# Ties, accumulator tiles and a layer border in a two-layer decoder trunk

## The chip, the core and the metric

The kernel runs on one core of one Trainium2 chip. The metric is device time in microseconds (us) of one execution, the median over a few runs. Engines are named as in the profile: PE is the tensor engine's matmul, PEld its weight load, DVE the vector engine, ACT the scalar engine, POOL the GpSimd engine, SP the engine that issues most of the loads.

## The reference

Two layers over x (256 positions x 2048 features), each `x <- LayerNorm(alpha * x + mixer(x))`:

```python
def reference(x, ...):
    for layer in range(DEPTH):                      # DEPTH = 2
        if layer % 2 == 0:
            h = ssd_moba_mixer(x, in0_w, ..., out0_w)
        else:
            h = s5_mixer(x, in1_w, ..., w_glu, out1_w)
        x = layer_norm(DEEPNORM_ALPHA * x + h, ln_g[layer], ln_b[layer])
    return x

def ssd_moba_mixer(x, w_in, conv_w, ...):
    z, xbc, dt, q, k, v, gate = jnp.split(x @ w_in, SPLITS0, axis=-1)
    xbc = jax.nn.silu(causal_depthwise_conv(xbc, conv_w, conv_b))
    ...                                             # SSD scan, causal attention
    return jnp.concatenate([y_a, y_b], axis=-1) @ w_out

def s5_mixer(x, w_in, ...):
    u, gate = jnp.split(x @ w_in, 2, axis=-1)
    y = jax.nn.gelu(s5_ssm(u, ...))                 # diagonal complex scan
    ga, gb = jnp.split(y @ w_glu, 2, axis=-1)
    return (ga * jax.nn.sigmoid(gb) * jax.nn.silu(gate)) @ w_out
```

All in float32. Nearly all arithmetic is in five projections: in0, out0, in1, glu, out1.

## The kernel before

**Split products.** Every float32 operand of a projection is split in two: a high part (`wh`, `xh`, rounded to the matmul's format) and the low rest (`wl`, `xl`). A product is the sum of three matmuls: high x high, high x low, low x high. Weights come in units of 256 rows x 512 columns (512 KB), 431 whole ones and a first one in parts. `split_to` (L210) loads a unit (`raw`, SP's queue), rounds it on ACT (L230) and subtracts on DVE (L232). `raw`, `wh` and `wl` have four buffers each, so a unit can be split once PE is done with the unit four before it.

**Products.** `product` (L288) runs over the units of one 512-column chunk. It calls `split_to` three units ahead, issues the unit's matmuls, and calls `pump`. Kind "w" (`wmm`, L273; 24 matmuls of 256 columns a unit, the weights stationary) gives a transposed result; kind "x" (`xmm`, L266; 12 matmuls of 512 columns a unit) a straight one. In kind "w" the two halves of the accumulator take turns within a unit (o = 0, 1 in the first bank, o = 2, 3 in the second). In order: 2 products for B and C, 4 for the convolution's x, 4 for z, 16 for attention, 4 of double length for out0, 8 for in1, 8 for glu, 4 for out1.

**Accumulators.** `banks` (L261) makes one tile of two PSUM banks for each product, of two tags in turn; `Pair` carries the tile and its halves. A product can start when the work that reads the tile of two products before is done.

**Spread work.** What follows from a product (convolution taps, rotary, scores, gates) is appended to `jobs`; longer-running work (SSD heads, the S5 tables' block jobs, the S5 scan) to `back`. `pump` (L242) calls a few of them after each unit, so that all of a product's `jobs` are traced during the next one. Each engine's final order is made by a planner that walks the program with a timing model: it takes work in traced order, but draws later work forward where it is ready and the engine would be idle. `tc.issue_after(ins)` makes the instructions of its block that run on the engine of `ins` come behind `ins` in that order. So far only `y_split` (L1175) uses it, against the split traced last, and the border's `step`.

**Early stage.** Product 3 to 6 are the convolution's x. After each, four taps (L498 on ACT, three L501 on DVE each) read the accumulator. Beside them run the softplus of dt (POOL, L451 to L462), the trigonometric and table jobs (L547 to L608) and, from far later in traced order, the first block job (`bars` L645 to L651, `efs` L665 to L675).

**Layer border.** `product_apart` (L323) computes out0's last chunk: ten units for both halves of the positions (t = 0, 1; o in the code), then the last six units first for t = 0 (36 matmuls) and then for t = 1. After each half, `after0` (L1019) queues its `first`: `res0` (L955: residual L960, statistics L961), `norm_stats` (L977 to L980, square root on ACT) and `step` (L994) for chunk 0; for t = 0 chunk 1 as well. A `step` takes 512 columns: L1003 and L1006 scale and shift on DVE, four transposes on PE (L351), the high part by a copy on ACT (L1014, tile C), the low part by a subtraction on DVE (L1015, tile F). Then come 60 small matmuls on a zero tile (`warm`, L356), and the first product of in1, whose unit k needs the columns 256k to 256k + 255 of both t. The remaining steps are traced inside that product (`later`), the one for t = 1, chunk 1 ahead of unit 1.

**End.** out1's last chunk uses `product_apart` too, with all eight units apart; `res1` (L1246: L1248, L1249) reads each half.

Of the kernel before, what the change touches and what calls it, by code (L numbers as in the profile page):

```python
# [9 lines left out]
F32 = mybir.dt.float32  # L10
# [6 lines left out]
P = 128  # L17
S = 256
# [7 lines left out]
WARM1 = 60  # L26
# [11 lines left out]

class Pair(list):
    def __init__(self, both, parts):  # L40
        super().__init__(parts)
        self.both = both

# [121 lines left out]
def trunk(tc, io, out):  # L165
# [8 lines left out]
    with ExitStack() as top:  # L174
# [32 lines left out]
        last = {}  # L207
        keep = [None, range(0)]

        def split_to(i):  # L210
            while nsplit[0] <= min(i, len(units) - 1):
                n = nsplit[0]
                if n in early:
                    early.pop(n)()
                raw = st.tile([P, UK, 512], F32, tag="raw", name=nm("raw"))
                if n == 0:
                    wh = st.tile([P, UK, 512], F32R, tag="wh", name=nm("wh"))
                    wl = st.tile([P, UK, 512], F32R, tag="wl", name=nm("wl"))
                    for k in range(UK):
# [10 lines left out]
                last["a"] = A.activation(wh, raw, AF.Copy)  # L230
# [10 lines left out]

        def pump(left):  # L242
            n = -(-len(jobs) // max(left, 1))
            for _ in range(n):
                jobs.popleft()()
            if back:
                goal[1] += len(back) / max(goal[0] - unit[0], 1)
            while back and goal[1] >= 1.0:
                back.popleft()()
                goal[1] -= 1.0  # L250

        def drain():
            while jobs:
                jobs.popleft()()

        def finish():
            while back:
                back.popleft()()
# [14 lines left out]
        def wmm(ps, u, nu, hl, wpair):  # L273
            pv = [p.rearrange("p (f n) -> p f n", n=S) for p in ps]
            wh, wl = wpair
            steps = [(j, o) for j in range(UK) for o in range(4)]
            if u == nu - 1:
                steps = [(j, o) for o in range(4) for j in range(UK)]
            for j, o in steps:
                first, end = u == 0 and j == 0, u == nu - 1 and j == UK - 1  # L280
                (xh, xl), k = hl(u * UK + j)
                sl = slice(o * P, o * P + P)
                for i, (l, r) in enumerate(((wh, xh), (wh, xl), (wl, xh))):
                    T.matmul(pv[o // 2][:, o % 2, :], l[:, j, sl], r[:, k, :],  # L284
                             start=first and i == 0 and o % 2 == 0, stop=end and i == 2 and o % 2 == 1,
                             skip_group_check=True)

        def product(kind, hl, nu=CU, prelude=None):  # L288
            ps = banks()
            for u in range(nu):  # L290
# [4 lines left out]
                if kind == "w":  # L295
                    wmm(ps, u, nu, hl, wpair)
# [26 lines left out]
        def product_apart(hl, nu, nk, after):  # L323
# [25 lines left out]
        def transpose4(dst, srcs):  # L349
            for i, s in enumerate(srcs):  # L350
                T.transpose(dst[:, i * P : i * P + P], s, ident)  # L351
# [630 lines left out]
        with ExitStack() as lt:  # L982
# [11 lines left out]
            def step(t, i, stats=None):  # L994
                if not x1t:
                    x1t["h"] = big("C", [P, KT, S], F32R)
                    x1t["l"] = big("F", [P, KT, S], F32R)
                sl = slice(512 * i, 512 * i + 512)
                xv = x1n[:, t, sl]
                with ExitStack() as pin:  # L1000
# [5 lines left out]
                    op2 = V.scalar_tensor_tensor(xv, xv, mr0[:, t, 2:3], rows[1][:, sl], op0=OP.mult, op1=OP.add)  # L1006
                tail["v"] = op2
                px = aux()
                transpose4(px, [x1n[:, t, (4 * i + f) * P : (4 * i + f) * P + P] for f in range(4)])
                pv = px.rearrange("p (f c s) -> p f s c", f=4, s=4)  # L1010
                fs = slice(4 * i, 4 * i + 4)
                hv = x1t["h"][:, fs, :].rearrange("p f (s c) -> p f s c", s=4)[:, :, :, 32 * t : 32 * t + 32]
                lv = x1t["l"][:, fs, :].rearrange("p f (s c) -> p f s c", s=4)[:, :, :, 32 * t : 32 * t + 32]
                A.activation(hv, pv, AF.Copy)  # L1014
                low = V.tensor_tensor(lv, pv, hv.bitcast(F32), op=OP.subtract)  # L1015
# [24 lines left out]
            first1 = product("w", x1hl, prelude=lambda u: [step(t, i) for t, i in later.get(u, [])])  # L1040
# [3 lines left out]
        with ExitStack() as l1:  # L1044
# [130 lines left out]
            def y_split(j):  # L1175
# [17 lines left out]
            for j in range(8):  # L1193
# [3 lines left out]
                else:  # L1197
                    jobs.append(lambda ps=ps, j=j: A.activation(sg1[:, :, 512 * j - 2048 : 512 * j - 1536], ps.both, AF.Silu))
# [10 lines left out]
            def glu_jobs(ps, j):  # L1209
                d = {}  # L1210

                def gate():
                    sb = w1("gt", [P, 2, 256])
                    A.activation(sb, ps.both[:, :, 256:512], AF.Sigmoid)
                    t1 = d["t"] = w1("p1", [P, 2, 256])
                    V.tensor_tensor(t1, ps.both[:, :, 0:256], sb, op=OP.mult)
# [81 lines left out]
```

## Time and profile before

| | us |
|---|---|
| median of 3 runs | 1376.59 |
| lowest, highest | 1375.08, 1376.98 |
| the profiled execution's own time | 1375.91 |
| its span in the profile | 1374.1 |
| its mean granted PE clock | 0.992 |

| engine | busy, us | share of the span |
|---|---|---|
| PE | 1346.6 | 98% |
| PEld | 1214.5 | 88% |
| DVE | 979.9 | 71% |
| ACT | 673.7 | 49% |
| POOL | 307.1 | 22% |

A line of the page's groups reads: source line, engine, operation, output <- inputs, shape, count | busy time, mean ns of one | idle time just before them and what ended it. A line of the view of waits reads: who waited <- for whom: us in total, times, longest. A row of the chain of waits or of the timeline begins with its start and its length in us; the chain follows the work that ended last back from the end. Matmuls overlap, so the pace of PE is read from starts, not from the length of one. The granted clock is the share of full speed that the tensor engine got.

### The profile page before, as it was taken

Reading aid. Unit: us, or ns where it says so; the run is one execution under the profiler, and the core shown is the slowest. Engines: PE = TensorE matmul, PEld = TensorE weight load, DVE = VectorE, ACT = ScalarE, POOL = GpSimd, SP = SyncE. Lnnn points to the kernel's source line nnn. Section 1 sums busy time; section 2 is a strip of 40 time slices with the busy share of each in tenths; the row PEclk is TensorE's granted clock in tenths of the full one; section 3 lists DMA queues with packets and bytes.
Section 4 is the critical chain, followed back from the end, with each engine's and each line's share of the span. In section 5 each row is a group of like instructions: output and inputs, shape, how many; then the busy total and the mean of one; then the engine's idle time right before and its main releaser. Section 6 shows DMA issues by size and latency. Waiting matters only on the chain.

```text
span 1374.1 us, 24912 instructions
## 1 busy us (share of the span) xinstructions
PE 1346.6 (98%) x9944; PEld 1214.5 (88%) x9944; DVE 979.9 (71%) x1548; ACT 673.7 (49%) x856; POOL 307.1 (22%) x457
## 2 busy tenths in 40 slices
PE   9996999999999999999999999899999999999996
PEld 9996999998999999999988888799977788888885
DVE  5789768888666679688768855748888846555555
ACT  5563557765554454454464434344344545444441
POOL 0157787833002002002000000023343200000001
PEclk9998999999999999999999999999999999999998
DMA  8554766555556656646756678387988766666761
GB/s 307 175 162 132 229 195 189 162 181 154 168 162 193 217 164 213 223 150 220 243 175 222 218 219 302 120 305 237 297 278 306 216 211 190 185 192 190 247 216 74
DMA packets 79204, 283.01 MB, mean 206 GB/s; under 512 B 9840, under 2 KB 10480, under 8 KB 78576
## 3 DMA queue, kind: packets, MB, share of 16 engines
q1 hardware_dynamic: 68112, 239.33, 55.4%
q0 software_dynamic: 10400, 40.90, 9.0%
q8 instruction: 78, 1.28, 0.4%
q10 hardware_dynamic: 576, 1.18, 0.2%
q14 instruction: 38, 0.31, 0.1%
HBM read 260.41 MB, written 20.97 MB: 205 GB/s over the span
## 4 chain that ended last, share of the span: by engine, by line
PE 91%; DVE 3%; DMA 2%; POOL 2%; ACT 1%; issue 1%; POOLq 0%; SPq 0%; DVEq 0%; ACTq 0%
PE main L271 42%; PE main L284 41%; DVE wl L232 1%; PE aux L351 1%; PE enc L1103 1%; PE aux L781 1%; DMA raw<-in_wo 1%; PE aux L687 1%; DMA raw<-in_wi 1%; PE aux L359 1%; DMA xr<-in_xn 1%; PE dec L1148 1%; POOL ew L461 1%; PE aux L683 1%; PE aux L861 1%
## 5 line engine op out<-in xcount | busy, mean ns | idle before, releaser
L232 DVE TENSOR_TENSOR wl<-raw,wh 128x1024 fp32r<-128x1024 f32 x431 | 540.7, 1259 | 281.2 <-ACT wh L230 275.2
L230 ACT ACTIVATE wh<-raw 128x1024 fp32r<-128x1024 f32 x431 | 455.4, 1059 | 549.4 <-PE main L271 272.5
L284 PE MATMUL main<-A,wh 128*128 128x256 f32 x1408 | 404.0, 287 | 10.3 <-DVE a L501 10.3
L284 PE MATMUL main<-A,wl 128*128 128x256 f32 x1408 | 400.8, 285 | 0.0
L284 PE MATMUL main<-B,wh 128*128 128x256 f32 x1408 | 400.2, 284 | 0.0
L284 PEld LDWEIGHTS main<-A,wh 128*128 128x128 f32 x1408 | 271.5, 193 | 11.2 <-issue 10.7
L284 PEld LDWEIGHTS main<-B,wh 128*128 128x128 f32 x1408 | 271.5, 193 | 0.3
L284 PEld LDWEIGHTS main<-A,wl 128*128 128x128 f32 x1408 | 271.5, 193 | 0.1
L271 PE MATMUL main<-wh,A 128*128 128x512 f32 x512 | 201.2, 393 | 1.7 <-DVE D L960 1.7
L271 PE MATMUL main<-wl,A 128*128 128x512 f32 x512 | 200.0, 391 | 0.0
L271 PE MATMUL main<-wh,B 128*128 128x512 f32 x512 | 199.6, 390 | 0.0
L271 PE MATMUL main<-wh,C 128*128 128x512 f32 x384 | 152.7, 398 | 0.8 <-DVE D L1248 0.8
L271 PE MATMUL main<-wl,C 128*128 128x512 f32 x384 | 149.9, 390 | 0.0
L271 PE MATMUL main<-wh,F 128*128 128x512 f32 x384 | 149.7, 390 | 0.0
L271 PEld LDWEIGHTS main<-wh,A 128*128 128x128 f32 x512 | 96.1, 188 | 22.2 <-DVE D L960 2.1
L271 PEld LDWEIGHTS main<-wh,B 128*128 128x128 f32 x512 | 96.1, 188 | 20.0
L271 PEld LDWEIGHTS main<-wl,A 128*128 128x128 f32 x512 | 96.2, 188 | 19.2
L271 PEld LDWEIGHTS main<-wh,C 128*128 128x128 f32 x384 | 72.1, 188 | 16.8 <-DVE D L1248 1.2
L271 PEld LDWEIGHTS main<-wh,F 128*128 128x128 f32 x384 | 72.1, 188 | 15.2
L271 PEld LDWEIGHTS main<-wl,C 128*128 128x128 f32 x384 | 72.1, 188 | 14.2
L284 PE MATMUL main<-C,wh 128*128 128x256 f32 x256 | 74.1, 290 | 0.7 <-ACT C L1014 0.7
L284 PE MATMUL main<-F,wh 128*128 128x256 f32 x256 | 73.5, 287 | 0.3 <-DVE F L1015 0.3
(281 smaller groups left out, 1575.6 us busy)
## 6 DMA issues: line engine op xcount, KB each, us to landing
raw<-in_wi SPq DMA_DIRECT2D x271, 512.0 KB, 4.2
raw<-in_wo SPq DMA_DIRECT2D x96, 512.0 KB, 4.2
raw<-in_wglu SPq DMA_DIRECT2D x64, 512.0 KB, 3.7
wt<-wb POOLq DMA_DIRECT2D x16, 896.0 KB, 7.7
wb<-ob POOLq DMA_DIRECT2D x16, 512.0 KB, 5.8
bc<-in_s5bc SPq DMA_DIRECT2D x16, 256.0 KB, 4.3
wb<-F POOLq DMA_DIRECT2D x16, 256.0 KB, 4.0
wb<-om POOLq DMA_DIRECT2D x16, 128.0 KB, 4.3
```

What stands on the lines that cost most here:

```text
L230: last["a"] = A.activation(wh, raw, AF.Copy)
L232: last["v"] = V.tensor_tensor(wl, raw, wh.bitcast(F32), op=OP.subtract)
L271: T.matmul(ps[o], l[:, k, sl], r[:, j, :], start=start and i == 0, stop=stop and i == 2)
L284: T.matmul(pv[o // 2][:, o % 2, :], l[:, j, sl], r[:, k, :], start=first and i == 0 and o % 2 == 0, stop=end and i == 2 and o % 2 == 1, sk ...
L351: T.transpose(dst[:, i * P : i * P + P], s, ident)
L359: T.matmul(px[:64, 0:64], idle, idle, start=i == 0, stop=i == n - 1)
L461: G.tensor_scalar(pl, pl, 1.0 / (2 * k + 1), None, op0=OP.add)
L683: T.transpose(pe[:, a * P : a * P + P], ev[:, a, :], ident)
L687: T.matmul(pk[at : at + 64, a * 16 : a * 16 + 16], ev[:, a, 64 * i : 64 * i + 64], cv[:, a, i, :], start=True, stop=True)
L781: T.matmul(yo, xs[:, 0, xc], df[:, i, 0:256], start=True, stop=False)
L861: T.matmul(px[:, 128:384], qT[:, h, P:S], kT[:, h, :], start=True, stop=True)
L1103: T.matmul(px[64 * at : 64 * at + 64, i, r * 128 + q * 64 : r * 128 + q * 64 + 64], wt[64 * i : 64 * i + 64, a * P + 64 * r : a * P + 64 * ...
```

## The change

Four things are changed.

1. **Ties.** Every spread job now runs through `run`, which puts its ACT and DVE instructions behind the split of the unit two ahead of the next one (or the last split traced). `splits` keeps each split's two instructions; the old tie in `y_split` goes.
2. **Accumulators.** `banks` makes two tiles of one bank each. What read both halves in one instruction (silu of the gate, sigmoid and product in `glu_jobs`) becomes two instructions.
3. **Order at the border.** `step` is cut in two, `scaled` (DVE) and `turned` (transposes, copy, subtraction). The t = 0 pieces' transposes are placed ahead of the last unit's matmuls of the second half (`mid`). For t = 1 chunk 0 is done in two pieces of 256 columns. The warm-up matmuls are 30 ahead of the first piece's transposes and 4 behind them. The second piece's transposes (`rest0`) come inside the first unit of in1.
4. **High parts first.** In that first unit, the two matmuls of each step that use the high part of x (`wh` x `xh`, `wl` x `xh`) are issued for all steps, then `rest0`, then those with the low part.

```diff
-WARM1 = 60
+WARM1 = 30
+WARM2 = 4
...
-                last["a"] = A.activation(wh, raw, AF.Copy)
+                high = A.activation(wh, raw, AF.Copy)
                 wl = pool.tile([P, UK, 512], F32R, tag=tl, name=nm("wl"))
-                last["v"] = V.tensor_tensor(wl, raw, wh.bitcast(F32), op=OP.subtract)
+                splits[n] = (high, V.tensor_tensor(wl, raw, wh.bitcast(F32), op=OP.subtract))
...
+        def run(job):
+            with ExitStack() as pin:
+                for ins in splits.get(min(unit[0] + 2, nsplit[0] - 1), ()):
+                    pin.enter_context(tc.issue_after(ins.ins))
+                job()
+
         def pump(left):
             n = -(-len(jobs) // max(left, 1))
             for _ in range(n):
-                jobs.popleft()()
+                run(jobs.popleft())
...
-            both = main.tile([P, 2, 512], F32, tag=f"m{turnno[0] % 2}", name=nm("main"))
-            return Pair(both, [both[:, o, :] for o in range(2)])
+            return [main.tile([P, 512], F32, tag=f"m{turnno[0] % 2}{o}", name=nm("main")) for o in range(2)]
...
-        def wmm(ps, u, nu, hl, wpair):
+        def wmm(ps, u, nu, hl, wpair, late=None):
...
+            for terms in ((0, 2), (1,)) if late else ((0, 1, 2),):
+                if late and terms == (1,):
+                    late()
+                for j, o in steps:
...
+                    for i in terms:
+                        l, r = ((wh, xh), (wh, xl), (wl, xh))[i]
+                        T.matmul(pv[o // 2][:, o % 2, :], l[:, j, sl], r[:, k, :],
...
-                    for j in range(UK):
-                        xmm(ps, o, ready[base + i], j, hl(u * UK + j), u == 0 and j == 0, u == nu - 1 and j == UK - 1)
+                    with ExitStack() as pin:
+                        if mid and o == 1 and i == nk - 1:
+                            pin.enter_context(tc.issue_after(mid().ins))
+                        for j in range(UK):
+                            xmm(ps, o, ready[base + i], j, hl(u * UK + j), u == 0 and j == 0, u == nu - 1 and j == UK - 1)
...
+            def turned(t, f0, nf):
...
+                px = aux()
+                end = transpose4(px, [x1n[:, t, f * P : f * P + P] for f in range(f0, f0 + nf)])
...
                 A.activation(hv, pv, AF.Copy)
-                low = V.tensor_tensor(lv, pv, hv.bitcast(F32), op=OP.subtract)
-                if (t, i) in ((0, 1), (1, 0)):
-                    tail["v"] = low
+                with ExitStack() as pin:
+                    if tail:
+                        pin.enter_context(tc.issue_after(tail["v"].ins))
+                    low = V.tensor_tensor(lv, pv, hv.bitcast(F32), op=OP.subtract)
+                return end, low
+
+            def step(t, i):
+                scaled(t, 4 * i, 4)
+                turned(t, 4 * i, 4)
...
-                    step(t, 0, norm_stats(st0, mr0, t))
+                    scaled(t, 0, 2 if t else 4, norm_stats(st0, mr0, t))
 
                 jobs.append(first)
-                if t == 0:
-                    jobs.append(lambda: step(0, 1))
-
-            product_apart(tailhl, 2 * CU, NKEEP, after0)
+                jobs.append((lambda: scaled(1, 2, 2)) if t else (lambda: scaled(0, 4, 4)))
+
+            def mid():
+                turned(0, 0, 4)
+                end, tail["v"] = turned(0, 4, 4)
+                return end
+
+            product_apart(tailhl, 2 * CU, NKEEP, after0, mid)
+            drain()
             warm(WARM1)
-            drain()
+            end, tail["v"] = turned(1, 0, 2)
+            with tc.issue_after(end.ins):
+                warm(WARM2)
...
+            def rest0():
+                tail["v"] = turned(1, 2, 2)[1]
...
-            first1 = product("w", x1hl, prelude=lambda u: [step(t, i) for t, i in later.get(u, [])])
+            first1 = product("w", x1hl, prelude=lambda u: [step(t, i) for t, i in later.get(u, [])], late=rest0)
...
-                with tc.issue_after(last["a"].ins), tc.issue_after(last["v"].ins):
-                    A.activation(y5["h"][:, fs, :], yt, AF.Copy)
-                    V.tensor_tensor(y5["l"][:, fs, :], yt, y5["h"][:, fs, :].bitcast(F32), op=OP.subtract)
+                A.activation(y5["h"][:, fs, :], yt, AF.Copy)
+                V.tensor_tensor(y5["l"][:, fs, :], yt, y5["h"][:, fs, :].bitcast(F32), op=OP.subtract)
```

More of the change, by code (lines that the diff above doesn't have):

```diff
@@ L37 @@
 GORDER = [16 * h + p + 8 * i for h in range(8) for p in range(8) for i in range(2)]
[L39 to L42, printed above, removed]
 CONST = {}
@@ L206, in trunk @@
         early = {}
-        last = {}
+        splits = {}
         keep = [None, range(0)]
@@ L248, in pump @@
             while back and goal[1] >= 1.0:
-                back.popleft()()
+                run(back.popleft())
                 goal[1] -= 1.0
@@ L253, in drain @@
             while jobs:
-                jobs.popleft()()
+                run(jobs.popleft())
         def finish():
             while back:
-                back.popleft()()
+                run(back.popleft())
             goal[1] = 0.0
@@ L278, in wmm, with product @@
                 steps = [(j, o) for o in range(4) for j in range(UK)]
[L279 to L288, printed above, removed]
+            for terms in ((0, 2), (1,)) if late else ((0, 1, 2),):
+                if late and terms == (1,):
+                    late()
+                for j, o in steps:
+                    first, end = u == 0 and j == 0, u == nu - 1 and j == UK - 1
+                    (xh, xl), k = hl(u * UK + j)
+                    sl = slice(o * P, o * P + P)
+                    for i in terms:
+                        l, r = ((wh, xh), (wh, xl), (wl, xh))[i]
+                        T.matmul(pv[o // 2][:, o % 2, :], l[:, j, sl], r[:, k, :],
+                                 start=first and i == 0 and o % 2 == 0, stop=end and i == 2 and o % 2 == 1,
+                                 skip_group_check=True)
+        def product(kind, hl, nu=CU, prelude=None, late=None):
             ps = banks()
@@ L295, in product @@
                 if kind == "w":
-                    wmm(ps, u, nu, hl, wpair)
+                    wmm(ps, u, nu, hl, wpair, late if u == 0 else None)
                 else:
@@ L321, in product_pair, with product_apart @@
                     between()
-        def product_apart(hl, nu, nk, after):
+        def product_apart(hl, nu, nk, after, mid=None):
             ps = banks()
@@ L350, in transpose4 @@
             for i, s in enumerate(srcs):
-                T.transpose(dst[:, i * P : i * P + P], s, ident)
+                end = T.transpose(dst[:, i * P : i * P + P], s, ident)
+            return end
         idle = cst.tile([P, 64], F32R, name="idle")
@@ L992, in trunk, with scaled @@
             tail = {}
[L994 to L998, printed above, removed]
+            def scaled(t, f0, nf, stats=None):
+                sl = slice(P * f0, P * (f0 + nf))
                 xv = x1n[:, t, sl]
@@ L1197, in trunk @@
                 else:
-                    jobs.append(lambda ps=ps, j=j: A.activation(sg1[:, :, 512 * j - 2048 : 512 * j - 1536], ps.both, AF.Silu))
+                    jobs.append(lambda ps=ps, j=j: [A.activation(sg1[:, t, 512 * j - 2048 : 512 * j - 1536], ps[t], AF.Silu) for t in range(2)])
                 if j == 0:
@@ L1213, in gate @@
                     sb = w1("gt", [P, 2, 256])
-                    A.activation(sb, ps.both[:, :, 256:512], AF.Sigmoid)
                     t1 = d["t"] = w1("p1", [P, 2, 256])
-                    V.tensor_tensor(t1, ps.both[:, :, 0:256], sb, op=OP.mult)
+                    for t in range(2):
+                        A.activation(sb[:, t, :], ps[t][:, 256:512], AF.Sigmoid)
+                    for t in range(2):
+                        V.tensor_tensor(t1[:, t, :], ps[t][:, 0:256], sb[:, t, :], op=OP.mult)
                     V.tensor_tensor(t1, t1, sg1[:, :, 256 * j : 256 * j + 256], op=OP.mult)
```

14 lines of the change are left out of this document (7 added, 7 removed).

## The prediction

> **What bounds the kernel now.** I read the page first, for the share of the tensor engine (PE), then the view of waits for PE alone, then the stretches around each wait (clock), and last the chain of waits through them.
>
> ```profile
> span 1374.1 us, 24912 instructions
> PE 1346.6 (98%) x9944; PEld 1214.5 (88%) x9944; DVE 979.9 (71%) x1548; ACT 673.7 (49%) x856; POOL 307.1 (22%) x457
> ```
>
> PE is busy for 1346.6 of 1374.1 us, so 27.5 us is all that PE stands still. Its waits:
>
> ```profile
> PE main L284 <- DVE a L501: 10.3, 1, 10.3
> PE main L271 <- DVE D L960: 1.7, 1, 1.7
> ...
> PE aux L351 <- DVE D L1006: 0.8, 1, 0.8
> PE main L271 <- DVE D L1248: 0.8, 1, 0.8
> PE main L284 <- ACT C L1014: 0.7, 1, 0.7
> PE main L284 <- DVE F L1015: 0.3, 1, 0.3
> ```
>
> One wait of 10.3 us (product 5 waits for the convolution taps that still read its accumulator), 1.7 us in the output projection, 0.8 + 0.7 + 0.3 us at the layer border, 0.8 us near the end: 14.6 us. The rest of the 27.5 is before the first and behind the last matmul, which the change leaves alone. No PE wait names a weight split, so the splits are early enough today. Standing still also costs clock afterwards:
>
> ```profile
> 109.50:119.86 10.36, 0.02 (x2) 0.04 (x1) 10.36 (x23) 1.58 (x3) 7.05 (x10) 0.72 0.54 166
> 119.86:124.00 4.14, 4.14 (x19) 4.14 (x20) 3.54 (x13) 2.72 (x3) 3.41 (x16) 0.50 0.24 96
> ...
> 881.50:885.50 4.00, 3.63 (x16) 3.43 (x17) 3.92 (x6) 0.00 (x0) 0.00 (x0) 0.57 0.00 0
> ```
>
> (Columns: stretch, length, busy time of PE, weight loads, DVE, ACT and POOL, granted clock, DMA share, GB/s.) Behind the long wait the clock is 0.50 for 4.14 us: 2.1 us lost. Behind the border it is 0.57 for 4 us: 1.7 us lost. So the long wait costs 10.3 + 2.1 = 12.4 us; these places together are all that the change can win.
>
> **Ties behind the splits.** Every spread job's ACT and DVE instructions are now issued behind the split three units ahead of the unit just traced. I compared where each job's instructions stand among the splits today: nearly all stand at or behind that split already. The exception are the S5 block jobs: they are traced after unit 104, yet the first block's DVE work runs at 109 us, among splits 33 to 35. The tie takes it out of the stretch that PE waits for:
>
> ```profile
> 108.79 0.66 DVE bb L645
> 109.45 0.53 DVE bb L647
> ...
> 115.09 0.20 DVE tm L646
> 115.29 0.26 DVE tm L648
> ...
> 116.18 0.17 DVE bb L649
> 116.35 0.20 DVE bb L650
> ...
> 118.55 0.52 DVE et L665 x2
> ...
> 119.19 0.23 DVE tm L666
> 119.41 0.31 DVE a L501
> ```
>
> DVE is busy for all 10.36 us of the wait, and the last tap (L501) ends it at 119.72. The eight block rows sum to 0.66 + 0.53 + 0.20 + 0.26 + 0.17 + 0.20 + 0.52 + 0.23 = 2.77 us, and with them gone the last tap ends that much sooner. Bounds: 0, if the planner fills the places with other work, and 12.4, if its new order puts the taps ahead of the table job that they now share DVE with. I take 2.77, since DVE's order among the rest has no reason to change. The block's work is done later, under the cover of PE's matmuls, at DVE's 71%. For the rest of the kernel I take the ties at 0; what hides them is that splits and jobs wait for PE and not PE for them (the rival below has the price if this cover is gone).
>
> **Separate accumulators.** Today both banks are one tile, so whoever reads one half holds back whoever writes the other. Three things follow. (a) Product 5 may start on bank 0 (taps 0 and 1, long done): unit 32 issues 6 matmuls there before it touches bank 1, at the pace of
>
> ```profile
> 900.40 24.23 PE main L284 x202
> ```
>
> 24.23/202 = 0.12 us each: 0.72 us of work moves into the wait. (b) The wait of 1.7 us on L960 is such a false one: PE is to write bank 1 while DVE reads bank 0. It goes, and so does (c) the 0.78 us on L1248 in the last product (0.8 in the waits). Bounds: 0 and these. What is late next: in (b) the t = 0 chain on DVE has the 36 matmuls of the second half in front of it and keeps its own times. The split evictions (sg1, gate) add an ACT and a DVE instruction per product, off the path; 0.
>
> **Layer border.** From the timeline of PE and the chain of waits, the rows between the second half's last matmul (its slot ends at 875.75, where the warm-up matmuls start) and the first matmul that nothing holds back:
>
> ```profile
> 875.52 0.39 PE L271 MATMUL main<-wh,B 128*128 128x512 f32 x1
> 875.75 3.63 PE L359 MATMUL aux<-idle 128*64 128x64 f32 x60
> ...
> 881.53 0.39 PE L284 MATMUL main<-C,wh 128*128 128x256 f32 x1 [0.69 <-ACT C L1014]
> ```
> ```profile
> 876.72 0.69 DVE D L960
> ...
> 878.62 0.66 DVE D L1003
> ...
> 879.38 0.76 DVE D L1006
> ...
> 880.19 0.67 PE aux L351 x4
> 880.88 0.60 ACT C L1014
> 881.51 0.70 DVE F L1015
> ...
> 882.26 4.56 PE main L284 x24
> 886.82 0.44 PE aux L351 x4
> ```
>
> That is 882.26 - 875.75 = 6.51 us. The operations on 256 columns do not exist here; the nearest are
>
> ```profile
> L757 ACT ACTIVATE b<-aux,cums 128x256 f32<-128x256 f32 x32 | 15.2, 474 | 4.2 <-PE aux L751 2.8 <-POOL a L842 1.4
> ...
> L501 DVE SCALAR_TENSOR_TENSOR a<-main,params,a 128x255 f32<-128x255 f32 x24 | 11.3, 473 | 0.5 <-ACT a L498 0.5
> ...
> L1003 DVE SCALAR_TENSOR_TENSOR D<-D,mr,row 128x512 f32<-128x512 f32 x8 | 6.0, 746 | 0.0
> ...
> L1014 ACT ACTIVATE C<-aux 128x512 fp32r<-128x512 f32 x8 | 4.5, 590 | 9.0 <-PE aux L351 9.0
> ```
>
> Step by step: DVE is still subtracting the t = 0 piece when the matmuls end; with its transposes moved ahead of the last 6 matmuls, L960 can start when the last matmul's record ends, 875.52 + 0.39 + 0.02 = 0.18 behind 875.75, instead of 0.97: 0.79 (bound 0). L1003 and L1006 on 256 columns: 2 x (0.746 - 0.473) = 0.55. Two transposes for four: half of 0.44, 0.2. ACT copy 0.590 - 0.474 = 0.12. High parts first: the subtraction leaves the path, 882.26 - 881.53 (the first matmul, behind the copy alone) = 0.73. Sum 2.4, so the first matmul comes 4.1 us behind the end. 30 warm-ups (half of 3.63 us) end before that.
>
> Not all of it stays. The next chunk's DVE work is pinned behind the second piece's subtraction, which needs 16 matmuls (1.9), two transposes (0.3), copy and subtraction (0.47 each) first, with hand-offs: 4.1 + 3.2 = 7.3 us behind the end. Today it starts when L1015 of 881.51 ends, at 882.2 or 6.5, and PE's fifth unit gets its low parts from
>
> ```profile
> 892.21 1.88 DVE L1015 TENSOR_TENSOR F<-aux,C 128x512 fp32r<-128x512 f32 x3
> ```
>
> done at 894.09, 18.3 behind the end. Later by 7.3 - 6.5 = 0.8, that is 19.1. PE wants them at 4.1 + 96 x 0.12 + 14 transposes (1.5) = 17.1 at full clock, 18.8 if the clock falls again; today it reaches that place at 6.5 + 1.7 + 11.5 + 1.5 = 21.2. So DVE, not the first matmul, sets the gain: 21.2 - 19.1 = 2.1. Bounds: 4.1 (clock kept, subtractions taken in good order), 0.5 (the 0.79 not won, and the additional switches).
>
> The clock: the gap of 1.7 us ahead of the second half kept it at 1.00,
>
> ```profile
> 866.60:873.70 7.10, 7.10 (x31) 5.83 (x32) 3.94 (x8) 0.20 (x1) 0.00 (x0) 1.00 0.62 192
> ```
>
> and the one of 5.8 us (875.75 to 881.53) lost it; 4.1 lies between. By the Trainium skill (TensorE: Matmul & The Clock Gate, Part 1) the gate falls after a whole idle window of a free-running 3.4 us; by that rule a gap of 4.1 mostly keeps it, and the sum would be the same, since DVE takes the 1.7 us back.
>
> **Sum.** 2.77 + 0.72 + 1.70 + 0.78 + 2.1 = 8.1 us. The profiled execution took 1375.9 us (span 1374.1 and 1.8 around it), 0.7 below the median of the three runs, 1376.6: 1375.9 - 8.1 = **1367.8 us**, its own range 1364 to 1370.
>
> **Rivals.** *The long wait goes altogether* (the planner orders DVE anew and the taps pass the table job): 12.4 instead of 2.77 + 0.72 = 3.5 there, 8.9 us more, 1358.9. For it: with four taps of 3 x 0.473 us the chain itself is short. Against it: all that the ties take out of the stretch is 2.77 us.
>
> *The early wait keeps its length* (freed DVE places are refilled by trig, table or phasor work), or the two tiles do not part PE from DVE, that is, the change does not do what it says: 1375.9 - (8.1 - 2.8) = 1370.6 or, without (a) to (c) alone, 1375.9 - (8.1 - 3.2) = 1371.0. For it: DVE has no idle time from 109.5 to 119.9.
>
> *Slower: strict order.* ACT stands behind splits that wait for PE, in the output products and others of this kind 170 times, and the split itself takes 1059 ns there:
>
> ```profile
> ACT wh L230 <- PE main L271: 272.5, 170, 2.7
> ```
> ```profile
> L230 ACT ACTIVATE wh<-raw 128x1024 fp32r<-128x1024 f32 x431 | 455.4, 1059 | 549.4 <-PE main L271 272.5
> ```
>
> A job that PE consumes (head pairs, attention turns, S5 encode and decode, some 96 in all) and that now sits behind such a split reaches PE late by up to one split, 1.06 us; PE runs its instructions in order, so all matmuls behind wait. One job in six makes 16 x 1.06 = 17 us: 1384.8. It decides from 8 such waits on. Against it: PE has not one such wait today, with the jobs at nearly the same places. The Trainium skill's page TensorE: Matmul & The Clock Gate (Part 1, queue depths) calls ACT and DVE strict FIFO; that is the rule that speaks against the change, and the trace agrees as far as the rows above go: ACT idles 549.4 us ahead of splits.
>
> **Chances.** Forecast 0.50; long wait gone 0.14; early wait kept or tiles without effect 0.24; strict order 0.12. A change within 0.2% (2.8 us) can't be told from none; only the last case lies outside: slower 0.10, same 0.04, faster 0.86. The range 1357 to 1374 holds the first three and leaves the slower case out.
>
> **What would show it.** Right: no block work (L645 to L668) among the taps, a wait on L501 of 6 to 7.5 us, none on L960 or on the last product's L1248, first border matmul 4 us behind the end, and then a wait on L1015's low parts or a clock near 0.5. Wrong: the wait on L501 gone or over 10 us; new PE waits on ACT or DVE between 125 and 830 us.

## The result, and the profile after

| | before | after |
|---|---|---|
| median, us | 1376.8 (12 runs) | 1373.03 (12 runs) |
| lowest, highest | 1374.97, 1379.2 | 1368.79, 1374.82 |
| ratio, 95% interval | | 0.9972 [0.9965, 0.9979] |
| the profiled execution's own time | 1375.91 | 1374.82 |

Faster by 3.8 us. The forecast was faster by 8 to 9, 1367.8. The profiled execution of after is the slowest of its twelve, so the accounts below, made on the two traces, add up to 1.1 us and not 3.8, and what they name as lost is larger than in a median run.

The page of after:

```profile
span 1373.0 us, 24879 instructions
...
PE 1349.7 (98%) x9918; PEld 1214.9 (88%) x9918; DVE 984.1 (72%) x1559; ACT 673.3 (49%) x869; POOL 295.0 (21%) x457
```

Its waits of PE (who waited <- for whom: total, times, longest):

```profile
PE dec L1171 <- DVE gt L1153: 3.7, 1, 3.7
PE dec L1167 <- ACT ys L1177: 2.5, 1, 2.5
PE aux L358 <- DVE D L1011: 1.8, 2, 1.3
PE main L288 <- DVE F L1025: 1.2, 1, 1.2
...
PE main L288 <- DVE a L509: 0.9, 1, 0.9
PE main L288 <- ACT C L1021: 0.3, 1, 0.3
```

The 10.3 us for the taps are 0.9 (taps are L509 now), the waits on `res0` (1.7) and on the last product's residual (0.8) are gone. New are 3.7 + 2.5 us in the S5 scan, where the kernel before had none, and the border's waits have moved from the first matmul to later ones. The stretches (length, then busy time of PE, weight loads, DVE, ACT and POOL, granted clock, DMA share, GB/s):

```profile
109.50:119.86 10.36, 9.47 (x80) 9.27 (x79) 10.14 (x20) 6.87 (x9) 6.32 (x7) 1.00 0.69 206
...
868.20:872.00 3.80, 3.74 (x19) 3.75 (x20) 0.43 (x2) 0.00 (x1) 0.00 (x0) 0.58 0.00 0
...
997.40:1004.00 6.60, 0.38 (x13) 0.24 (x12) 4.38 (x6) 4.16 (x5) 3.48 (x6) 0.84 0.64 157
1004.00:1010.00 6.00, 6.00 (x54) 4.93 (x55) 4.47 (x7) 0.04 (x1) 0.56 (x1) 0.61 0.82 262
```

The first row is the stretch in which PE stood for 10.3 us before: now it works at full clock. The second is the border, at 0.58. The last two are the new stall, PE still for 6.2 of 6.6 us, and the lower clock behind it.

To see where the time went I compared when PE starts the matmul at the same place of the same product in both traces (the projections have 7680 in each). Difference of after to before, in us:

| stretch | what changed there | change |
|---|---|---|
| products 4 to 6 | the wait for the taps and the clock behind it | -11.3 |
| attention and out0 | small shifts both ways | +1.7 |
| last product of out0 and border | `res0`'s wait, border | -1.6 |
| in1 and S5 scan, to glu | the new stall and the clock behind it, 8.7; small steps, 2.3 | +11.1 |
| last product | wait on the last residual, end | -1.1 |

So the gain came, larger than forecast, and most of it was lost again 890 us later.

**The stall.** The chain of waits of after, in order of time (start, length, what):

```profile
989.33 9.18 DMA ut<-yd
...
998.53 1.07 ACT A L1204
...
999.62 0.04 DVE B L1205
999.66 1.10 issue
1000.76 1.29 DVE p L1138 x2
...
1003.30 0.62 DVE gt L1153
1003.92 0.04 issue
1003.97 0.83 PE dec L1171 x16
```

`y_load` brings a piece of the scan's output back; `y_split` (L1204 on ACT, L1205 on DVE) splits it. The load lands at 998.5. Until then ACT stands behind L1204 and DVE behind L1205. Behind L1205 is queued the next recurrence step of the scan (rotation L1138, L1153), for which PE's `dec` matmuls wait (3.7 us); behind L1204 is queued ACT's copy of the scan's result before (L1177), for which they wait too (2.5 us). The idle times, ACT's row first, then DVE's, on their timelines:

```profile
998.53 1.06 ACT L1204 ACTIVATE A<-ut 128x1024 fp32r<-128x1024 f32 x1 [10.13 <-DMA ut<-yd]
```
```profile
999.62 1.23 DVE L1205 TENSOR_TENSOR B<-ut,A 128x1024 fp32r<-128x1024 f32 x1 [8.36 <-ACT A L1204]
```

In the kernel before the order on DVE is scan, rotation, split, then `y_split`: ACT waited 5.9 us for the same load and PE not at all.

```profile
1004.74 1.06 ACT L1182 ACTIVATE A<-ut 128x1024 fp32r<-128x1024 f32 x1 [5.86 <-DMA ut<-yd]
```

Both `y_split` and the recurrence job `rec2` are tied behind the same weight split now, and `y_split` comes first in the list of its step.

### The profile page after: what moved, and what is told of

It reads as the page before. It is cut to its first block, busy times and chain, and to the rows that moved or that the text cites. A ratio compares the mean times of both kernels' runs of the same rounds, so it can differ in the third digit from the quotient of the medians.

```text
span 1373.0 us, 24879 instructions
## 1 busy us (share of the span) xinstructions
PE 1349.7 (98%) x9918; PEld 1214.9 (88%) x9918; DVE 984.1 (72%) x1559; ACT 673.3 (49%) x869; POOL 295.0 (21%) x457
## 4 chain that ended last, share of the span: by engine, by line
PE 92%; DVE 3%; POOL 2%; issue 1%; DMA 1%; ACT 1%; POOLq 0%; DVEq 0%
PE main L271 44%; PE main L288 40%; DVE wl L227 1%; PE aux L358 1%; PE aux L789 1%; PE aux L695 1%; DMA ut<-yd 1%; PE enc L1126 1%; PE dec L1171 1%; PE aux L367 1%; POOL ew L469 1%; PE aux L901 1%; PE aux L691 1%; PE aux L869 1%; PE aux L759 0%
## 5 line engine op out<-in xcount | busy, mean ns | idle before, releaser
L288 PE MATMUL main<-C,wl 128*128 128x256 f32 x256 | 73.4, 287 | 0.0
```

Of the source, the lines that this page charges most:

```text
L288: T.matmul(pv[o // 2][:, o % 2, :], l[:, j, sl], r[:, k, :], start=first and i == 0 and o % 2 == 0, stop=end and i == 2 and o % 2 == 1, sk ...
```

## The experiments

All times of an experiment stand beside the kernel before on the same chip (1375.97, 1377.14, 1375.75 and 1376.9 us in the four sets).

**Each part alone.** `tiles`: on the kernel before, `banks` and the three places that used both halves at once, nothing else.

```diff
-            both = main.tile([P, 2, 512], F32, tag=f"m{turnno[0] % 2}", name=nm("main"))
-            return Pair(both, [both[:, o, :] for o in range(2)])
+            return [main.tile([P, 512], F32, tag=f"m{turnno[0] % 2}{o}", name=nm("main")) for o in range(2)]
```

> The kernel before with the two separate accumulator tiles alone. Theory A (the tiles end the early wait, since the taps of the two banks no longer wait for each other between ACT and DVE): PE's wait for the taps falls from 10.3 us to under 1.5 us, the waits on the residual of the second half are gone, no PE wait in the S5 stage: 11.4 + 1.9 + 0.8 us less than 1376.8, 1362.7 us (1361 to 1365). Rival B (the ties end it): the early wait stays at 9 to 10.3 us and the time is 1373 to 1375 us. Rival C for the new wait in the S5 stage (PE is ahead of the data's round trip through DRAM, however it got ahead): PE waits there for 5 us or more, 1368 to 1373 us.

`ties`: on the kernel before, `splits`, `run` and its calls, and `y_split` without its old tie.

```diff
-                jobs.popleft()()
+                run(jobs.popleft())
...
-                back.popleft()()
+                run(back.popleft())
```

> The kernel before with the ties alone. Theory A: the early wait shrinks by the 2.8 us of block work only, to 7 to 8 us; and theory D (the tie puts the second rotation of an S5 block behind the split of the round trip's data) has PE wait in the S5 stage for 3 us or more with a lower clock behind it: 1374 to 1384 us, not faster than before. Rival B: the early wait is under 2 us. Rival C: PE is not ahead here, so no wait in the S5 stage: 1373 to 1375 us.

`border`: the new order at the border alone (`scaled`, `turned`, `mid`, `rest0`, 30 and 4 warm-up matmuls), one tile, no ties.

> The kernel before with the new layer border alone: one two-bank accumulator tile, no ties. Theory (the gain of the new kernel comes from the separate accumulators, and the border gives almost nothing because its half clock also delays VectorE's chain): within 2 us of the kernel before, 1374.0 to 1376.5, the wait of 10.3 us for the taps unchanged, the clock between 862 and 873 us below 0.9. Rival (the border is worth the 2.1 us that the prediction gave it, and loses them only to the ties): 1373.2 to 1374.2 with no wait of TensorE behind the first half.

| | median, us (lowest, highest) | ratio to before [95%] |
|---|---|---|
| tiles | 1366.07 (1364.49, 1366.97) | 0.9923 [0.9908, 0.9937] |
| ties | 1385.51 (1381.86, 1386.67) | 1.0061 [1.0044, 1.0077] |
| border | 1376.93 (1374.41, 1378.04) | 0.9998 [0.9989, 1.0008] |

The tiles alone win some 10 us, the ties alone lose some 9, the border is worth nothing. Two times lie outside what was expected: `tiles` is 1 us above its 1361 to 1365 (PE has a new wait of 2.1 us for a weight split there, and loses time at the border, see below), `ties` 1.5 us above its 1374 to 1384. (In `border` everything comes later, and the half clock stands in the stretch 873 to 884, 0.85, not in the one that the expectation named.)

What the tiles do is seen on their timeline, ACT's taps first, then the first two and last two taps of DVE for the same product:

```profile
89.20 0.57 ACT L497 ACTIVATE a<-main,params 128x256 f32<-128x256 f32 x1
...
89.80 0.58 ACT L497 ACTIVATE a<-main,params 128x256 f32<-128x256 f32 x1
```
```profile
89.88 0.48 DVE L500 SCALAR_TENSOR_TENSOR a<-main,params,a 128x255 f32<-128x255 f32 x1
...
90.48 0.48 DVE L500 SCALAR_TENSOR_TENSOR a<-main,params,a 128x255 f32<-128x255 f32 x1
...
103.64 0.47 DVE L500 SCALAR_TENSOR_TENSOR a<-main,params,a 128x253 f32<-128x253 f32 x1
...
104.93 0.47 DVE L500 SCALAR_TENSOR_TENSOR a<-main,params,a 128x253 f32<-128x253 f32 x1
```

Two feature blocks, one in each bank, are worked on side by side, and all twelve taps are done at 105.4, four us before PE wants the tile at 109.5. In the kernel before the blocks went strictly one after the other, ACT's first tap of each waiting for DVE's last of the one before, and the last tap ended at 119.7:

```profile
97.92 0.56 ACT L498 ACTIVATE a<-main,params 128x256 f32<-128x256 f32 x1 [1.15 <-DVE a L501]
104.35 0.56 ACT L498 ACTIVATE a<-main,params 128x256 f32<-128x256 f32 x1 [2.44 <-DVE a L501]
110.87 0.56 ACT L498 ACTIVATE a<-main,params 128x256 f32<-128x256 f32 x1 [3.20 <-DVE a L501]
```

In the view of ACT's waits these are part of one row:

```profile
ACT a L498 <- DVE a L501: 20.5, 11, 4.2
```

Its size does not show what the order costs PE: in `tiles` ACT waits for DVE's taps as long, 22.4 us in 9 waits, and PE not at all.

The Trainium skill (PSUM — Partial Sum Buffer, section on bank collisions) says that two engines must not touch one bank and quadrant at once, reads against reads included, and that the back end sets a dependency between them. The traces agree, and show more: with one tile of two banks also the blocks in different banks were kept apart. What sets the dependency in these kernels the traces do not show.

The ties alone have this list of PE waits (that kernel is 6 lines longer, so the taps are L507 and the scan's lines L1136 to L1160):

```profile
PE main L290 <- DVE a L507: 6.5, 1, 6.5
PE dec L1154 <- DVE gt L1136: 3.7, 1, 3.7
PE main L277 <- DVE D L966: 1.9, 1, 1.9
PE dec L1150 <- ACT ys L1160: 1.5, 1, 1.5
...
```

The taps' wait is 6.5, 3.8 less than before where the prediction gave the ties 2.77, and the S5 stall is there with one tile as well: it belongs to the ties.

**Is it y_split?** `noties`: after without the ties (`run` only calls the job; `y_split` keeps its old tie). `ylate`: after, `y_split` one step of the schedule later:

```diff
-                    at(2 * b + 8, lambda b=b: y_split(b // 4))
+                    at(2 * b + 9, lambda b=b: y_split(b // 4))
```

> The changed kernel without the ties (the split of the S5 result keeps the tie that it had before). Theories A and D: early wait under 1.5 us, no PE wait in the S5 stage, border as in the changed kernel: 1376.8 - 11.4 - 1.5 - 0.8 = 1363.1 us (1361 to 1366). Rival B: early wait back at 9 us or more, 1371 to 1374 us. Rival C: S5 wait of 5 us or more stays, 1369 to 1374 us.

> The changed kernel with the split of each S5 result (y_split) one step later in the spread work, ties kept. Theory D: the block's second rotation comes ahead of it on DVE, PE's waits of 6.2 us on the S5 decode go, with the clock loss behind them: 1363 to 1366 us, and less spread from run to run than the 6 us of the changed kernel. Rival C: PE waits elsewhere in the S5 stage for as long, 1370 to 1374 us.

`noties` took 1365.41 us (1363.27 to 1366.04), 0.9915 [0.9898, 0.9931]; `ylate` 1365.11 (1364.76 to 1366.05), 0.9918 [0.9903, 0.9933]. Neither has a wait of PE in the scan, and both lie in the range expected. One step of one job gives back some 7.5 us (0.9972 against 0.9918).

**Do the ties cost elsewhere?** `tieslate` is `ties` with the same step added.

> The kernel before with the ties alone and y_split one step later (the ties alone took 1385.5 us). Theory (the ties take four microseconds off the early wait, 10.3 to 6.5, and cost something at one place only, the step in which y_split stands ahead of the second rotation): no wait of TensorE between 985 and 1010 us, 3 to 4.5 us less than before, 1372 to 1373.5. Rival (a strict order behind the splits costs a little in many places): the early wait is 6.5 all the same, and the time 1375 to 1380.

It took 1378.62 us (1375.54 to 1381.21), 1.0018 [1.0009, 1.0028]: the rival holds. By the positions of the matmuls it gains 3.6 us at the taps and no S5 stall is left, yet it ends 3.3 behind the kernel before. From attention through out0 it loses 1.3 us in small shifts. Over in1 and the scan it loses some 3 us in steps of 0.3 to 0.4: with the ties PE's program runs the scan's `dec` matmuls in 22 groups, without them in 16; on the timeline a `dec` group of 48 takes 0.86 us whole, 0.28 + 0.75 in two parts, and the large matmuls behind each part start anew. (0.7 us of the 3 are one wait for a weight load.) And in the last product of out0 it loses 2 us: DVE reaches `res0` later, and the clock falls behind the wait. The same wait in `ties`, on PE's timeline:

```profile
863.73 0.52 PE L277 MATMUL main<-wh,A 128*128 128x512 f32 x1 [1.86 <-DVE D L966]
```

and the stretches with it and behind it:

```profile
860.67:864.08 3.41, 1.55 (x8) 0.96 (x7) 2.92 (x4) 2.34 (x2) 0.00 (x0) 1.00 0.88 263
864.08:867.49 3.41, 3.41 (x10) 2.67 (x9) 3.27 (x8) 0.20 (x1) 0.00 (x0) 0.50 0.95 328
```

Here 1.86 us of idling, 2.2 in `tieslate`, cost half the clock for 3.4 us (the matmuls start 0.42 us apart instead of 0.23); 1.71 in the kernel before and 1.80 in `border` cost none. It is not the length of the wait alone. In `noties` PE idles 2.1 us from 284.45 on, waiting for a weight split, and keeps the clock:

```profile
282.56:285.97 3.41, 1.89 (x16) 1.24 (x14) 3.41 (x6) 3.38 (x7) 1.72 (x3) 1.00 0.00 0
285.97:289.38 3.41, 2.81 (x23) 2.82 (x24) 3.41 (x8) 2.25 (x3) 0.00 (x0) 1.00 0.48 144
```

In all traces of this case the granted clock changes only on a grid of 3.41 us: each stretch at 0.50 or 1.00 lasts a whole multiple of it, other than those that the kernel's start and end cut off. The waits of `ties` and `tieslate` lie within one step of the grid; those that cost nothing are divided by a boundary, 1.53 + 0.59 us in `noties`, 0.85 + 0.95 in `border`, 0.16 + 1.54 before. The first full clock comes 10.5 to 13.7 us into the span, in each execution at another place, so where a wait falls on the grid is luck, and with it part of these 2 us.

**Why do the tiles end the wait: the hand-overs, or the first bank?** `inits` keeps one tile, and puts ACT's four first taps of a product in one job ahead of DVE's twelve, so that the engines change once and not four times.

```diff
...
-                        A.activation(acc[:, f, :], src, AF.Identity, bias=cb[:, ft + f : ft + f + 1], scale=cw[:, ft + f, 3:4])
...
-                jobs.extend([tap(f) for f in range(4)])
+                def inits():
+                    for f in range(4):
+                        src = ps[f // 2][:, (f % 2) * S : (f % 2) * S + S]
+                        A.activation(acc[:, f, :], src, AF.Identity, bias=cb[:, ft + f : ft + f + 1], scale=cw[:, ft + f, 3:4])
+
+                jobs.extend([inits] + [tap(f) for f in range(4)])
```

> The kernel before, one two-bank accumulator tile, no ties, old border; only the order of the taps is changed: the four first taps of a product, ScalarE's, are one job ahead of the twelve taps of VectorE, instead of one ahead of each three. Theory (with one tile ScalarE's and VectorE's reads of it exclude each other, and each change from one engine to the other is a wait in a queue; the early stage pays it eight times in a product, 20.5 us of ScalarE's idling in all): the early wait of TensorE for the taps falls from 10.3 us to 4 or less, 6 us less than before or more, 1367 to 1370. Rival (the separate tiles gain because TensorE may start on the first bank while VectorE still reads the second): TensorE still needs the whole tile, the wait stays between 8 and 11, 1374 to 1377.

1373.65 us (1371.26 to 1377.62), 0.998 [0.997, 0.999], and

```profile
PE main L284 <- DVE a L500: 8.1, 1, 8.1
```

My number fell: 8.1, not 4; the 8 to 11 of the rival holds. But the rival's cause does not explain `tiles`, for there the whole tile is free before PE wants it. In after, with tiles and ties, it does count:

```profile
113.41 0.39 PE L288 MATMUL main<-A,wh 128*128 128x256 f32 x1 [0.89 <-DVE a L509]
```
```profile
112.88 0.47 DVE L509 SCALAR_TENSOR_TENSOR a<-main,params,a 128x253 f32<-128x253 f32 x1
```

PE starts product 5 at 109.48 and issues 24 matmuls before it waits: in its program the planner has put the matmuls of units 32 and 33 that write the first bank ahead of those that write the second. Had PE needed the whole tile, it would have waited 3.9 us. So of the 9.4 us that the wait became shorter, 6.4 come from the earlier end of the last tap (113.35 instead of 119.71) and 3.0 from the first bank.

What goes with the end of the last tap is how much stands in DVE's queue ahead of it. Counted in DVE's program, for the product that PE waits for:

| | place of the last tap in DVE's queue | other instructions between first and last tap | of them S5 block work | PE's wait for it, us |
|---|---|---|---|---|
| before | 155 | 49 | 10 | 10.3 |
| ties | 141 | 38 | 0 | 6.5 |
| inits | 141 | 31 | 2 | 8.1 |
| after | 135 | 32 | 0 | 0.9 |
| tiles | 131 | 26 | 0 | 0 |

The planner draws work forward where an engine would be idle, so a tap that can't start yet has other work put ahead of it, and in a queue that stays ahead. Two chains side by side would leave fewer such holes; that this is the reason is argued, not shown. The place alone does not give the wait: `ties` and `inits` have the same, 141, with 6.5 and 8.1 us. With `inits` the chain is short but begins later (first tap at 96.7 us, 89.9 in `tiles`), and why the planner starts it there is open.

**The border.** Three edits on `ylate` (1365.1 us). `wide`: idle matmuls of 512 columns in place of those of 64, 12 and 2 of them. `fill`: the scaling of the next chunk, two DVE instructions, ahead of `rest0`'s subtraction, where DVE is idle. `widefill`: both.

```diff
-WARM1 = 30
-WARM2 = 4
+WARM1 = 12
+WARM2 = 2
...
-            warm(WARM1)
+
+            def wide(n):
+                px = aux()
+                for i in range(n):
+                    T.matmul(px[:64], idle, yah[:, 2 * (i % 4) : 2 * (i % 4) + 2, :].rearrange("p k s -> p (k s)"), start=i == 0, stop=i == n - 1)
+
+            wide(WARM1)
...
-                warm(WARM2)
+                wide(WARM2)
```
```diff
             def rest0():
+                scaled(1, 4, 4)
                 tail["v"] = turned(1, 2, 2)[1]
...
-            first1 = product("w", x1hl, prelude=lambda u: [step(t, i) for t, i in later.get(u, [])], late=rest0)
+            first1 = product("w", x1hl, prelude=lambda u: [turned(1, 4, 4) if u == 1 else step(t, i) for t, i in later.get(u, [])], late=rest0)
```

> The new kernel with y_split one step later (1365.1 us), and at the border the 30 and 4 idle matmuls of 64 columns replaced by 12 and 2 of 512 columns. Theory (the gap filled with short matmuls and 1.3 us of idling is what halves the clock, and the half clock costs 1.6 us on TensorE and as much on VectorE's chain): clock 1.00 between 862 and 873, the sixteen high-part matmuls in about 1.9 us instead of 3.5, and 1.5 to 2 us less, 1363.1 to 1363.6. Rival one (the clock is lost whatever fills the gap): no change, 1365.1. Rival two (VectorE's chain sets the border, so that the clock is bought back as waits): clock 1.00 but waits of TensorE for L1011 and L1025 longer by as much, 1364.8 to 1365.3.

> The new kernel with y_split one step later (1365.1 us), and the scaling of token tile 1's second chunk of 512 columns, two instructions of 0.75 us, put ahead of rest0's subtraction, where VectorE stands idle for 3.95 us. Theory (VectorE's chain behind rest0 sets the two later waits of TensorE at the border, 0.66 and 1.34 us): both waits go or shrink below 0.3, 1.3 to 2 us less, 1363.1 to 1363.8. Rival (the chain is set by something else, the weight splits of ScalarE or the transposes): waits of the same length elsewhere, 1364.8 to 1365.3.

> Both edits of the two runs before on the new kernel with y_split one step later. Theory: the two gains add, 3 to 3.7 us less than 1365.1, 1361.4 to 1362.1, clock 1.00 and no wait of TensorE above 0.5 us between 862 and 890 but those of the gap itself. Rival (one shortage behind both): no more than the better of the two alone, about 1363.3.

The medians are near what a few runs can tell apart, so the stretch itself is read on PE's timelines: from the start of the second half's last matmul to that of matmul 181 of in1, when the border's waits are over.

| | border, us | median, us | ratio to before [95%] |
|---|---|---|---|
| before | 31.9 | | |
| border | 32.3 | 1376.93 | 0.9998 [0.9989, 1.0008] |
| tiles | 33.9 | 1366.07 | 0.9923 [0.9908, 0.9937] |
| after | 32.3 | 1373.03 | 0.9972 [0.9965, 0.9979] |
| ylate | 32.4 | 1365.11 | 0.9918 [0.9903, 0.9933] |
| wide | 30.9 | 1364.49 | 0.9909 [0.9893, 0.9926] |
| fill | 29.7 | 1362.68 | 0.9901 [0.9886, 0.9916] |
| widefill | 28.4 | 1362.44 | 0.9894 [0.988, 0.9909] |

After, PE's timeline of the gap:

```profile
864.19 1.88 PE L367 MATMUL aux<-idle 128*64 128x64 f32 x30
867.35 0.44 PE L358 MATMUL aux<-consts,D 128*128 128x128 f32 x2 [1.27 <-DVE D L1011]
867.54 0.45 PE L367 MATMUL aux<-idle 128*64 128x64 f32 x4
868.26 0.39 PE L288 MATMUL main<-C,wh 128*128 128x256 f32 x1 [0.27 <-ACT C L1021]
...
877.00 0.63 PE L358 MATMUL aux<-consts,D 128*128 128x128 f32 x4 [0.55 <-DVE D L1011]
...
879.30 0.39 PE L288 MATMUL main<-F,wh 128*128 128x256 f32 x1 [1.24 <-DVE F L1025]
```

DVE there:

```profile
868.24 0.42 DVE L1025 TENSOR_TENSOR F<-aux,C 128x256 fp32r<-128x256 f32 x1
872.52 0.42 DVE L1025 TENSOR_TENSOR F<-aux,C 128x256 fp32r<-128x256 f32 x1 [3.86 <-ACT C L1021]
872.86 0.74 DVE L1008 SCALAR_TENSOR_TENSOR D<-D,mr,row 128x512 f32<-128x512 f32 x1
```

The first matmul starts 868.26 - 864.19 = 4.07 us behind the end, but at half clock: the 16 high-part matmuls take 3.2 us, and `rest0`'s transposes behind them start at 871.44. So DVE idles 3.86 us, the pinned scaling starts at 872.86, and PE meets its results late twice, 0.55 and 1.24 us. With wide idle matmuls the same stretch is

```profile
868.40:872.40 4.00, 3.98 (x34) 3.97 (x34) 1.52 (x4) 0.94 (x2) 0.00 (x0) 1.00 0.00 0
```

at full clock, which is worth 1.5 us of the border; the two later waits stay as long as they were (0.7 and 1.4), against the second rival. The median falls by 0.6 us only, between what the theory and that rival gave. With both edits DVE reads

```profile
868.52 0.74 DVE L1008 SCALAR_TENSOR_TENSOR D<-D,mr,row 128x512 f32<-128x512 f32 x1
869.30 0.75 DVE L1011 SCALAR_TENSOR_TENSOR D<-D,mr,row 128x512 f32<-128x512 f32 x1
871.04 0.42 DVE L1025 TENSOR_TENSOR F<-aux,C 128x256 fp32r<-128x256 f32 x1 [0.98 <-ACT C L1021]
```

the scaling done in the idle time, and the two later waits are gone. The border is 2.7 us shorter with `fill` alone, where 1.3 to 2 were expected, and 4.0 with both, where 3 to 3.7 were expected; the medians fall by 2.4 and 2.7.

`tiles` has the longest border: PE's second half of out0 begins 1.9 us earlier there and, as the eight transposes that ran inside it now follow it, ends 2.9 us earlier; 2.0 of that are lost at the old border, and 0.6 more in a wait inside in1.

**A version that beats both.** `nowf`: `noties` with the two edits of the border.

> The changed kernel without ties (y_split keeps its old one), with the two edits of the border (wide idle matmuls, second scaling ahead of rest0's subtraction) that brought the tied version to 1362.4 us. Theory (with separate accumulators the early wait is gone with or without ties, so that the ties are worth nothing): within 1.5 us of 1362.4. Rival (the ties are still worth the 3 to 4 us that they take from the early wait with one tile): 1365 to 1366.

1360.8 us (1359.9 to 1362.14), 0.9888 [0.9872, 0.9905]: 15 us below the kernel before, 12 below the changed one, a little more than the 1.5 us expected below `widefill`. Beside `widefill` (0.9894) that is no difference: at the early products the ties spare PE waits for weight splits (3.0 us in `nowf`), and from attention to the scan they cost about as much.

## Why the prediction was wrong

The direction was right, every wait that it named moved, and the size was off by more than half: 8.1 us forecast, 3.8 measured, out of one gain that was taken too small and one loss that was taken at nothing.

- **Ties, 2.77 us at the taps: right in kind, too small.** The block work (L645 to L668 before) is gone from the stretch, and with the ties alone the wait is 6.5 us: 3.8 less than before. (The 6 to 7.5 announced had the 0.72 of the tiles in it.)
- **Separate accumulators, (a) 0.72 us: the mechanism was missed.** The step counted only that PE may begin on the first bank, with 6 matmuls; in the planned order it is 24, 3.0 us, beyond the bound that it set. And the tiles also let the taps of the two banks run side by side: alone they end the wait, with the last tap at 105.4. With both changes the last tap moves from place 155 to 135 in DVE's queue, and the wait ends almost wholly: with the clock 11.3 us, not 3.5. The rival of the long wait going altogether had this size (12.4) with another cause.
- **(b) and (c): the waits went as forecast,** 1.7 and 0.8 us. (c) is kept to the end. (b) can't be added to the border: in `tiles` most of it is lost there again.
- **Border, 2.1 us: the step "the sum would be the same" with or without the clock failed.** The first matmul came 4.07 us behind the end, 4.1 forecast, and DVE's chain sets the gain, as said. But its second subtraction stands behind 16 matmuls on PE, so the half clock delays the chain itself: the pinned scaling started 8.7 us behind the end, not 7.3. Border and (b) together gave 1.6 us where 3.8 were counted; with the clock kept and the scaling moved they give 4.7 (`widefill`, by matmul positions).
- **"For the rest of the kernel I take the ties at 0": this is the step that cost the forecast.** 11.1 us were lost over in1 and the scan, 8.7 of them in the one stall with its clock; by the medians of after and `ylate` the stall costs some 7.5. The rival of strict order had the mechanism, a job behind a place in a queue that PE then waits for, but spread over sixteen places and behind weight splits; most of it was one place, behind a load that lands late. The rest is small: 2.3 us in the scan, which `ylate` loses too (2.2), and 1.7 from attention through out0. The cover named in the prediction, that splits wait for PE and not PE for them, says nothing of the order among the tied jobs themselves, and that is what changed.

## What to carry to other kernels

When a tie or a priority changes the order of work in a queue, look for the instruction in it that waits longest (a load, not an ALU operation) and ask what is now behind it; the share of busy time says nothing of that. An accumulator that two engines read should be one tile for each bank; here that alone gave 0.9923. What shows it is the order of the readers on the timeline, one block after the other, and not the size of their waits. A gap at a border costs twice if the engine that idles also feeds the one that sets the end: keep its clock with matmuls like those of the product, and give the other engine something that is due anyway.

## What was not expected of the hardware

The prediction cites the rule that the clock falls after a whole idle window of a free-running 3.4 us (the Trainium skill, TensorE: Matmul & The Clock Gate, Part 1). The traces show the window, as the grid of 3.41 us, but less idling is enough. Among matmuls of full width, 1.86 us (`ties`) and 2.24 us (`tieslate`) of idling within one step halved the clock for the next; 1.54 us (before) did not, nor did 1.80 and 1.89 us at the ends of `tieslate` and `tiles`, so the edge lies near 1.9 us. By the same rule the prediction expected the border gap of 4.1 us to keep the clock mostly; it did not in any run with narrow idle matmuls.

These do not count like wide ones. In the step of `tiles` from 864.74 to 868.15 PE idles 0.82 us only and runs idle matmuls of 64 columns for the rest, and the clock falls behind it; before, 1.54 us of idling among matmuls of 512 columns kept it. So in the border gap, where 34 matmuls of 64 columns did not keep the clock (0.58) and 14 of 512 columns did (1.00), the 1.3 us of idling that the wide ones remove are not the whole reason. Whether their width counts or their data was not tried apart: the narrow ones multiply zeros by zeros, the wide ones have activations on one side.
